# Channel mixing by Strassen's seven block products, with the activations in DRAM

## The chip, the cores and the metric

One core of a Trainium2 chip runs the whole kernel in one launch. The metric is the device time of one execution in microseconds (us). TensorE (PE) multiplies; VectorE (DVE), ScalarE (ACT) and GpSimd (POOL) do the elementwise work; the queue of SyncE (SP) issues most transfers.

## The reference, cut to what matters

One decoder layer for 1024 tokens of width 1024. The change concerns the second half, after the residual add of the mixing part:

```
x = x + gt1[:, None, :] * (merged @ w_out[l])
h2 = _modulate(x, norm2_g[l], sh2, sc2)
ff_out = jnp.square(jax.nn.relu(h2 @ w_ff1[l])) @ w_ff2[l]
x = x + gt2[:, None, :] * ff_out
return _rmsnorm(x, final_g)
```

h2 is 1024 x 1024, w_ff1 1024 x 4096 ("up"), w_ff2 4096 x 1024 ("down"), everything in float32.

## The kernel before, in words

Every float32 product is made of three fp32r matmuls: each operand is split into a high part (hi, an ACT cast) and a low part (lo = raw - hi, a DVE subtraction), and PE adds hi·hi, lo·hi and hi·lo in PSUM. An operand tile so costs one ACT and one DVE operation.

The mixing half fills the first 1036 us. Its last step is w_out: for each of eight token blocks t, 96 matmuls into `p_out`, then DVE forms x1 = x + gt1 * p_out in tile `xr`, SP stores it to `x1_d` in DRAM, ACT squares it, a chain of small operations (`rsqrt`, seven DVE and ACT operations on one column) gives the row scale, DVE scales `xr`, and after four blocks PE transposes (`hp`), ACT applies the conditioning (`hr`) and each 128x512 piece is split into `hhi` and `hlo`: h2 transposed, kept in SBUF.

The channel half goes by 32 column blocks n of 128. `up(n)` loads a block of w_ff1 (`load_w`, split into wh and wl), multiplies (48 matmuls of 512 columns), and makes relu squared as a split pair `fh`, `fl`. `w2(n)` loads the matching 128 rows of w_ff2, POOL multiplies them by gt2, and ACT and DVE split them. `down(g)` takes two n at a time (four in the last) and for each token block and each half of the columns adds the products of n in one PSUM bank `o`; DVE adds it to `acc[t]`, which was loaded with x1. In the last group `finish(t)` normalises a block as soon as it is complete and stores it. Ups and downs alternate in program order, two ups ahead. Each engine runs its instructions in the order in which the scheduler has put them.

## Time and profile before

| | |
|---|---|
| median of 3 runs | 1753.14 us (1746.7 to 1756.55) |
| profiled execution, its own time | 1749.61 us |
| its span in the trace | 1747.6 us |
| PE busy | 1671.4 us, 96% |
| DVE busy | 971.1 us, 56% |
| ACT busy | 570.3 us, 33% |
| POOL busy | 368.3 us, 21% |
| first up matmul / last down matmul begins | 1036.9 / 1739.40 us |

The times of single operations come from the profiled execution, 3.5 us under the median. Busy shares are means over the whole span; those of a stretch are read from the windows below.

### The profile page before, as it was taken

How to read it: one execution, taken by the hardware profiler on the slowest of the kernel's cores; microseconds unless marked ns; L12 is line 12 of the kernel's file. 1: busy time of each engine (PE TensorE's matmuls, PEld its weight loads, DVE VectorE, ACT ScalarE, POOL GpSimd, SP SyncE). 2: the span in 40 equal slices, each digit the busy share in tenths (PEclk: the TensorE clock that was granted, in tenths of full speed). 3: DMA queues.
4: the chain of work that ended last, by engine and by line, in shares of the span. 5: the costliest groups of instructions: out<-in, count | busy, mean ns of one | idle time of the engine just before them, and what ended most of it. 6: DMA issues, size and time to landing. Idle time of an engine off the chain costs nothing.

```text
span 1747.6 us, 21804 instructions
## 1 busy us (share of the span) xinstructions
PE 1671.4 (96%) x8677; PEld 1350.8 (77%) x8677; DVE 971.1 (56%) x1500; ACT 570.3 (33%) x869; POOL 368.3 (21%) x265
## 2 busy tenths in 40 slices
...
GB/s 249 126 112 154 109 99 161 121 61 61 67 70 103 73 232 240 249 235 232 248 204 247 75 125 137 49 48 49 48 49 49 49 49 49 48 49 48 37 12 96
DMA packets 205907, 197.50 MB, mean 113 GB/s; under 512 B 28113, under 2 KB 170730, under 8 KB 205678
## 3 DMA queue, kind: packets, MB, share of 16 engines
...
q10 hardware_dynamic: 208, 0.28, 0.0%
HBM read 148.80 MB, written 43.09 MB: 110 GB/s over the span
## 4 chain that ended last, share of the span: by engine, by line
PE 81%; DVE 5%; DMA 4%; ACT 2%; issue 1%; POOL 0%; SPq 0%; DVEq 0%; ACTq 0%
PE o L41 20%; PE p_f L41 20%; PE p_gb L41 5%; PE p_out L41 4%; PE p_ga L41 3%; PE my L41 3%; PE p_ob L41 2%; PE p_fq L41 2%; PE p_fv L41 2%; PE p_fk L41 2%; PE p_v L41 2%; PE yv L41 2%; PE p_r L41 2%; PE p_k L41 2%; PE tp L818 2%; PE s L41 1%
## 5 line engine op out<-in xcount | busy, mean ns | idle before, releaser
L1193 DVE TENSOR_TENSOR acc<-acc,o 128x512 f32<-128x512 f32 x240 | 162.1, 686 | 193.8 <-PE o L41 193.8
L1157 POOL TENSOR_TENSOR w2r<-w2r,gt 128x1024 f32<-128x1024 f32 x32 | 77.3, 2431 | 721.8 <-DMA w2r<-in_w_ff 721.7
L41 PE MATMUL p_f<-hlo,wh_f 128*128 128x512 f32 x512 | 200.0, 391 | 0.0
L41 PE MATMUL p_f<-hhi,wl_f 128*128 128x512 f32 x512 | 199.6, 390 | 0.0
L41 PE MATMUL p_f<-hhi,wh_f 128*128 128x512 f32 x512 | 199.5, 390 | 0.0
L41 PE MATMUL o<-w2h,fl 128*128 128x512 f32 x496 | 193.4, 390 | 0.0
L41 PE MATMUL o<-w2l,fh 128*128 128x512 f32 x496 | 193.2, 390 | 0.0
L41 PE MATMUL o<-w2h,fh 128*128 128x512 f32 x496 | 193.0, 389 | 0.0
L1143 ACT ACTIVATE rl<-p_f 128x1024 f32<-128x1024 f32 x32 | 32.9, 1028 | 268.4 <-PE p_f L41 268.4
L177 DVE TENSOR_TENSOR wl_f<-wr_f,wh_f 128x1024 fp32r<-128x1024 f32 x32 | 41.1, 1284 | 142.3 <-ACT wh_f L176 142.3
L1163 ACT CAST w2h<-w2r 128x1024 fp32r<-128x1024 f32 x31 | 31.1, 1050 | 251.4 <-PE o L41 251.4
L41 PEld LDWEIGHTS p_f<-hlo,wh_f 128*128 128x128 f32 x512 | 96.1, 188 | 20.4 <-DVE hlo L1124 0.5
L41 PEld LDWEIGHTS p_f<-hhi,wl_f 128*128 128x128 f32 x512 | 96.1, 188 | 20.2
L41 PEld LDWEIGHTS p_f<-hhi,wh_f 128*128 128x128 f32 x512 | 96.1, 188 | 20.0
L41 PEld LDWEIGHTS o<-w2h,fl 128*128 128x128 f32 x496 | 93.1, 188 | 20.0
L41 PEld LDWEIGHTS o<-w2h,fh 128*128 128x128 f32 x496 | 93.1, 188 | 19.8
L41 PEld LDWEIGHTS o<-w2l,fh 128*128 128x128 f32 x496 | 93.1, 188 | 19.5
L638 POOL TENSOR_TENSOR dg<-dg,inv 128x62 f32<-128x62 f32 (+30 forms) x62 | 100.2, 1616 | 4.8
L637 POOL TENSOR_TENSOR inv<-dg 128x62 f32<-128x62 f32 (+30 forms) x62 | 93.0, 1500 | 4.9
L822 DVE TENSOR_TENSOR pl<-tp,ph 128x512 fp32r<-128x512 f32 (+1 forms) x80 | 49.2, 632 | 24.8 <-ACT ph L821 24.6
L700 POOL TENSOR_TENSOR sw<-sbd,wcs 64x256 f32<-64x256 f32 x28 | 22.9, 818 | 168.0 <-DVE sbd L701 137.5
L880 ACT ACTIVATE pt<-pt,sm 128x128 f32<-128x128 f32 (+3 forms) x64 | 49.5, 775 | 24.5 <-DVE sm L878 23.5
...
## 6 DMA issues: line engine op xcount, KB each, us to landing
...
```

The source lines that it names most:

```text
L41: PE.matmul(o, l, r, start=start, stop=stop)
L177: DVE.tensor_tensor(lo, raw, hi.bitcast(F32), ALU.subtract)
L637: POOL.tensor_tensor(tv, dg[:, 0:s, s : s + 1].broadcast_to([P, s, m]), dg[:, s : s + 1, s + 1 :].broadcast_to([P, s, m]), ALU.mult)
L638: POOL.tensor_tensor(dg[:, 0:s, s + 1 :], dg[:, 0:s, s + 1 :], tv, ALU.add)
L700: POOL.tensor_tensor(sw[rs], cur[rs, :, rs], wcs[rs, :, c : c + 1].broadcast_to([64, 4, 64]), ALU.mult)
L818: PE.transpose(tp[:, x * P : (x + 1) * P], pr[b][:, t * P : (t + 1) * P], ident)
L822: DVE.tensor_tensor(pl[:, 0:w_], tp[:, 0:w_], ph[:, 0:w_].bitcast(F32), ALU.subtract)
L880: ACT.activation(pt[:, 0:n], pt[:, 0:n], AF.Exp, bias=low, scale=-1.0, accum_out=ls[:, b : b + 1])
L1143: ACT.activation(rl, o, AF.Relu)
L1157: POOL.tensor_tensor(raw, raw, gt2, ALU.mult)
L1163: ACT.copy(wh, raw)
L1193: DVE.tensor_tensor(acc[t][:, sl], acc[t][:, sl], o, ALU.add)
```

## The change

Strassen's scheme in Winograd's form splits each matrix product into 2 x 2 blocks and makes seven block products in place of eight, for sums of blocks before and after.

**Up.** The 32 column blocks go in 16 pairs j. The inner dimension is cut in two halves of four 128-row tiles, the tokens in two halves, the pair in its two blocks. On the side of h2 four sums T1 to T4 are built once, for each k of four by three POOL and three DVE sums and five splits (`t0` to `t3`, `hx`, and T3 and B22 written over parts of hhi and hlo). On the side of the weights each pair needs S1 to S4 (four POOL sums of 128x512) and seven splits. A pair takes 7 x 12 = 84 matmuls for 96. Four result blocks `ff0` to `ff3` of a pair, 128x512, are put together from PSUM banks x, y, z by ACT copies and DVE adds, go through relu squared, and are stored to `f_d` in DRAM. The products that need only h2's first token half (`up_first`, x and z) are issued around the sums T.

**Down.** After all ups, four groups g of eight column blocks go through seven steps each. A step is one block product: four token blocks t, 12 matmuls of 512 columns each. Four A blocks (activations, from `f_d`) and four B blocks (w_ff2), 128x2048 each (1 MB), are loaded per group, each tile once per group; POOL makes S1 to S4 and T1 to T4 at 128x2048, and each step splits its two operands (slots for two steps). Results go from PSUM to `acc` (the first time by an ACT copy, later by DVE). gt2 and x1 are applied to acc in the last group (`close_half`), then `finish`.

The diff, cut to its core; code of w_out that has only moved is left out:

```diff
+    def raw_pair(j):
+        tiles = []
+        for d in range(2):
+            if j % 3 == 0:
+                r = wp.tile([P, 4, 2 * P], F32, tag="wraw", name=f"ur{j}_{d}", bufs=2)
+            else:
+                r = dpr.tile([P, 4, 2 * P], F32, tag="dr", name=f"ur{j}_{d}", bufs=4)
+            SP.dma_start(r, ff1[:, 4 * d : 4 * d + 4, 2 * P * j : 2 * P * (j + 1)])
+            tiles.append(r)
+        return tiles
...
+    def split(hi, lo, src):
+        ACT.copy(hi, src)
+        DVE.tensor_tensor(lo, src, hi.bitcast(F32), ALU.subtract)
...
+        if t == 3:
+            for k in range(KT):
+                hp_ = turn(0, k, "ps")
+                hr = dpr.tile([P, 512], F32, tag="dr", name=f"hr2{t}_{k}", bufs=4)
+                ACT.activation(hr, hp_, AF.Identity, bias=sh2[:, k : k + 1], scale=sc2[:, k : k + 1])
+                split(hhi[:, k, 0:512], hlo[:, k, 0:512], hr)
+            raw1[0] = raw_pair(0)
+            for d in (1, 0):
+                first_ops(0, d)
...
+    psum_pools(x=(4, 512), y=(2, 512), z=(2, 512))
+    hxh, hxl = [hx.tile([P, 3, 4, 512], F32R, name=f"hx{x}") for x in "hl"]
+    blk = lambda t_, d, g: t_[:, 4 * d : 4 * d + 4, 512 * g : 512 * g + 512]
+    HB = {
+        "B11": (blk(hhi, 0, 0), blk(hlo, 0, 0)),
+        "B21": (blk(hhi, 1, 0), blk(hlo, 1, 0)),
+        "B22": (blk(hhi, 1, 1), blk(hlo, 1, 1)),
+        "T3": (blk(hhi, 0, 1), blk(hlo, 0, 1)),
...
+    def up_product(o, w, b, start):
+        (wh, wl), (bh, bl) = w, HB[b]
+        for k in range(4):
+            mmx(o, wh[:, k], bh[:, k], start and k == 0, False)
+            mmx(o, wl[:, k], bh[:, k], False, False)
+            mmx(o, wh[:, k], bl[:, k], False, k == 3)
...
+    def f_store(j, b, sq=None):
+        f = Fb[j, b]
+        DVE.scalar_tensor_tensor(f, f, 0.0, f, ALU.max, ALU.mult)
+        SP.dma_start(f_d[b, j], f)
...
+            z = bank(f"z{j}", "z")
+            up_product(z, (wh[:, 4:8], wl[:, 4:8]), "B21", True)
+            ACT.copy(f_tile(j, 0), z)
+        else:
+            X[j] = bank(f"x{j}", "x")
+            up_product(X[j], (wh[:, 0:4], wl[:, 0:4]), "B11", True)
+            DVE.tensor_tensor(Fb[j, 0], X[j], Fb[j, 0], ALU.add)
+            f_store(j, 0)
...
+    for k in range(4):
+        hr = dpr.tile([P, 2, 512], F32, tag="dr", name=f"hr3{k}", bufs=4)
+        for i in range(2):
+            hp_ = turn(4, k + 4 * i, "y")
+            ACT.activation(hr[:, i], hp_, AF.Identity, bias=sh2[:, k + 4 * i : k + 4 * i + 1], scale=sc2[:, k + 4 * i : k + 4 * i + 1])
+        h12, h22 = hr[:, 0], hr[:, 1]
+        tt = [tq.tile([P, 512], F32, name=f"t{x}_{k}", tag=f"hxt{x}", bufs=1) for x in range(4)]
+        f32 = lambda b, i: HB[b][i][:, k].bitcast(F32)
+        DVE.tensor_tensor(tt[0], h12, f32("B11", 0), ALU.subtract)
+        DVE.tensor_tensor(tt[0], tt[0], f32("B11", 1), ALU.subtract)
+        POOL.tensor_tensor(tt[2], h22, h12, ALU.subtract)
+        split(HB["T1"][0][:, k], HB["T1"][1][:, k], tt[0])
+        DVE.tensor_tensor(tt[1], h22, tt[0], ALU.subtract)
+        split(HB["T2"][0][:, k], HB["T2"][1][:, k], tt[1])
+        split(HB["B22"][0][:, k], HB["B22"][1][:, k], h22)
+        POOL.tensor_tensor(tt[3], f32("B21", 0), tt[1], ALU.subtract)
+        POOL.tensor_tensor(tt[3], tt[3], f32("B21", 1), ALU.add)
+        split(HB["T3"][0][:, k], HB["T3"][1][:, k], tt[2])
+        split(HB["T4"][0][:, k], HB["T4"][1][:, k], tt[3])
+        up_first(k // 2, k % 2 == 0)
+    tops.close()
...
+        made = {
+            "S1": (a21, a22, ALU.add),
+            "S2": (src, a11, ALU.subtract),
+            "S4": (a12, src, ALU.subtract),
+            "S3": (a11, a21, ALU.subtract),
+        }.get(name)
+        if made:
+            POOL.tensor_tensor(src, *made)
+        wh, wl = [up_.tile([P, 4, P], F32R, name=f"{name}{x}_{j}", tag=f"wop{x}", bufs=5) for x in "hl"]
+        split(wh, wl, src)
+        rest[j, name] = wh, wl
...
+        if i == 0:
+            y = X[j, "y"] = bank(f"y{j}", "y")
+            up_product(y, rest.pop((j, "S1")), "T1", True)
+            ACT.copy(f_tile(j, 3), y)
+        elif i == 1:
+            up_product(x, rest.pop((j, "S2")), "T2", False)
+            ACT.copy(f_tile(j, 1), x)
+        elif i == 2:
+            up_product(X[j, "y"], rest.pop((j, "S4")), "B22", False)
+            DVE.tensor_tensor(Fb[j, 1], X[j, "y"], Fb[j, 1], ALU.add)
+            f_store(j, 1)
+        elif i == 3:
+            up_product(x, rest.pop((j, "S3")), "T3", False)
+            DVE.tensor_tensor(Fb[j, 3], x, Fb[j, 3], ALU.add)
+            f_store(j, 3)
+        else:
+            up_product(x, rest.pop((j, "A22")), "T4", False)
+            ACT.activation(f_tile(j, 2), x, AF.Relu)
+            f_store(j, 2)
...
+    for j in range(NPAIR):
+        if j + 2 < NPAIR:
+            raw1[j + 2] = raw_pair(j + 2)
+        for i in range(5):
+            if i == 4 and j + 2 < NPAIR:
+                up_first(j + 2, True)
+            up_step(j, i)
+            if j + 1 < NPAIR:
+                rest_op(j + 1, ORDER[i])
+            if j + 2 < NPAIR and i in (1, 2):
+                first_ops(j + 2, 2 - i)
+        if j + 2 < NPAIR:
+            up_first(j + 2, False)
...
-        def up(n):
-            o = proj(load_w(ff1[:, :, n * P : (n + 1) * P], 0, KT, f"f{n}"), f"p_f{n}")
-            rl = fp.tile([P, S], F32, name=f"rl{n}", tag="rl", bufs=2)
-            ACT.activation(rl, o, AF.Relu)
-            if n < NFF - 1:
-                fh = fp.tile([P, S], F32R, name=f"fh{n}", tag="fh", bufs=3)
-                fl = fp.tile([P, S], F32R, name=f"fl{n}", tag="fl", bufs=3)
-            else:
-                fh, fl = [wp.tile([P, S], F32R, name=f"f{x}{n}", tag="wraw", bufs=2) for x in "hl"]
-            ACT.activation(fh, rl, AF.Square)
-            DVE.tensor_tensor(rl, rl, rl, ALU.mult)
-            DVE.tensor_tensor(fl, rl, fh.bitcast(F32), ALU.subtract)
-            return fh, fl
-        def w2(n):
-            raw = fp.tile([P, D], F32, name=f"w2r{n}", tag="w2r", bufs=2)
-            SP.dma_start(raw, ff2[n])
-            POOL.tensor_tensor(raw, raw, gt2, ALU.mult)
-            if n < NFF - 1:
-                wh = fp.tile([P, D], F32R, name=f"w2h{n}", tag="w2h", bufs=3)
-                wl = fp.tile([P, D], F32R, name=f"w2l{n}", tag="w2l", bufs=3)
-            else:
-                wh, wl = [wp.tile([P, D], F32R, name=f"w2{x[-1]}{n}", tag=x, bufs=2) for x in ("whi", "wlo")]
-            ACT.copy(wh, raw)
-            DVE.tensor_tensor(wl, raw, wh.bitcast(F32), ALU.subtract)
-            return wh, wl
...
+            t_ = raws[name] = fp.tile([P, 4, 512], F32, name=f"{name}_{g}", tag=name, bufs=1)
+            i = int(name[2])
+            if name[0] == "A":
+                b = {"11": 0, "12": 2, "21": 1, "22": 3}[name[1:]]
+                src = f_d[b, 4 * g : 4 * g + 4].rearrange("j p n -> p j n")
+            else:
+                n, d = {"11": (0, 0), "12": (0, 1), "21": (1, 0), "22": (1, 1)}[name[1:]]
+                src = ff2[:, 8 * g : 8 * g + 8].rearrange("p (j i) n -> p j i n", i=2)[:, :, n, 512 * d : 512 * d + 512]
+            SP.dma_start(t_, src)
...
+                POOL.tensor_tensor(R["S"], R["A21"], R["A22"], ALU.add)
...
+        STEPS = [
+            ("y", True, "A12", "B21", [(0, 0)]),
+            ("x", True, "A11", "B11", [(0, 0)]),
+            ("y", True, "S", "T", [(1, 1)]),
+            ("x", False, "S", "T", [(0, 1)]),
+            ("y", False, "S", "B22", [(0, 1)]),
+            ("x", False, "A21", "B12", [(1, 1)]),
+            ("x", False, "A22", "T", [(1, 0)]),
+        ]
+        SUMS = [(), (), ("S1", "T1"), ("S2", "T2"), ("S4",), ("S3", "T3"), ("T4",)]
+        LOADS = [("A12", "B21"), ("A11", "B11"), ("A21", "A22", "B12"), ("B22",), (), (), ()]
...
+                hi, lo = [fp.tile([P, 4, 512], F32R, name=f"{x}{y}{g}_{i}", tag=f"op{x}{y}", bufs=2) for y in "hl"]
+                split(hi, lo, raws[name])
...
+            if (t, d) in seen:
+                DVE.tensor_tensor(acc[t][:, sl], o, acc[t][:, sl], ALU.add)
+            else:
+                seen.add((t, d))
+                ACT.copy(acc[t][:, sl], o)
...
+            x1t = fp.tile([P, 512], F32, name=f"x1t{t}_{d}", tag="x1t", bufs=4)
+            SP.dma_start(x1t, x1_d[t][:, sl])
+            a_ = acc[t][:, sl]
+            DVE.tensor_tensor(a_, a_, gt2[:, sl], ALU.mult)
+            DVE.tensor_tensor(a_, a_, x1t, ALU.add)
+            jk = fp.tile([P, 512], F32, name=f"jk3{t}{d}", tag="jk3", bufs=1)
+            ACT.activation(jk, a_, AF.Square, accum_out=ssq[:, 8 * d + t : 8 * d + t + 1])
...
-                    o = bank(f"o{g}_{t}_{hf}")
-                    for i in range(n):
-                        (fh, fl), (wh, wl) = fs[i], ws[i]
-                        mm(o, fh[:, ts_], wh[:, sl], i == 0, False)
-                        mm(o, fl[:, ts_], wh[:, sl], False, False)
-                        mm(o, fh[:, ts_], wl[:, sl], False, i == n - 1)
-                    DVE.tensor_tensor(acc[t][:, sl], acc[t][:, sl], o, ALU.add)
...
+        flat = [(g, i) for g in range(NG) for i in range(7)]
+        operands(*flat[0])
+        for s, (g, i) in enumerate(flat):
+            if s + 1 < len(flat):
+                operands(*flat[s + 1])
+            tag, opens, _, _, to = STEPS[i]
+            (fh, fl), (wh, wl) = ops.pop((g, i))
+            for t in range(4):
+                ts_ = slice(t * P, t * P + P)
+                if opens:
+                    banks[tag, t] = bank(f"{tag}{g}_{i}_{t}", tag)
+                o = banks[tag, t]
+                for j in range(4):
+                    mmx(o, fh[:, j, ts_], wh[:, j], opens and j == 0, False)
+                    mmx(o, fl[:, j, ts_], wh[:, j], False, False)
+                    mmx(o, fh[:, j, ts_], wl[:, j], False, j == 3)
+                for half, d in to:
+                    evict(o, t + 4 * half, d)
+                if g == NG - 1:
+                    if i == 4:
+                        close_half(t, 0)
+                        close_half(t, 1)
+                        finish(t)
+                    elif i == 5:
+                        close_half(t + 4, 1)
+                    elif i == 6:
+                        close_half(t + 4, 0)
+                        finish(t + 4)
```

In program order PE has the same rows as before up to the last p_out matmul but for the names of transposes; in all it has 7007 rows for 7391. Three places in the order, `L` being the line in each kernel's own file:

DVE, before, from the scaling of the last token block on; `hr27_k` is the k-th piece of the second token half, then the splits of weights and activations of the first ups follow:

```order
L1113 TENSOR_SCALAR xr7_8978<-xr7_8978,rs2_8407 128x1024
L1124 TENSOR_TENSOR hlo_125<-hr27_0_8998,hhi_124 128x512
L1124 TENSOR_TENSOR hlo_125<-hr27_1_9007,hhi_124 128x512
...
L1124 TENSOR_TENSOR hlo_125<-hr27_7_9061,hhi_124 128x512
L177 TENSOR_TENSOR wl_f2_9231<-wr_f2_9228,wh_f2_9230 128x1024
L1150 TENSOR_TENSOR rl0_9145<-rl0_9145 128x1024
```

DVE, after, from the same place on, then the end of that stretch; `hr3k` holds two pieces, `S1l_0` is the low part of the first S1 of pair 0, on which the first matmul into bank `y0` waits:

```order
L1153 TENSOR_SCALAR xr7_8994<-xr7_8994,rs2_8413 128x1024
L1234 TENSOR_TENSOR t0_0_9054<-hr30_9041,hhi_124 128x512
L1235 TENSOR_TENSOR t0_0_9054<-t0_0_9054,hlo_125 128x512
L1238 TENSOR_TENSOR t1_0_9055<-hr30_9041,t0_0_9054 128x512
L1104 TENSOR_TENSOR hlo_125<-hr30_9041,hhi_124 128x512
L1104 TENSOR_TENSOR hxl_9029<-t0_0_9054,hxh_9028 128x512
L1104 TENSOR_TENSOR hlo_125<-t2_0_9056,hhi_124 128x512
L1104 TENSOR_TENSOR hxl_9029<-t1_0_9055,hxh_9028 128x512
...
L1104 TENSOR_TENSOR uwlo2_9310<-ur2_0_9265,uwhi2_9309 128x512
L1104 TENSOR_TENSOR hxl_9029<-t1_3_9200,hxh_9028 128x512
L1104 TENSOR_TENSOR hxl_9029<-t3_3_9202,hxh_9028 128x512
L1104 TENSOR_TENSOR S1l_0_9243<-S_0_9240,S1h_0_9242 128x512
```

Where eight subtractions for hlo stood ahead of the first weight split, 38 rows now stand up to and with `S1l_0`; one of them is an add from PSUM, the other 37 take both inputs from SBUF.

POOL, before, in the channel half: one row for each n, 32 in all, of which these are the first:

```order
L1157 TENSOR_TENSOR w2r0_9214<-w2r0_9214,gt2_5349 128x1024
L1157 TENSOR_TENSOR w2r1_9221<-w2r1_9221,gt2_5349 128x1024
L1157 TENSOR_TENSOR w2r2_9480<-w2r2_9480,gt2_5349 128x1024
L1157 TENSOR_TENSOR w2r3_9487<-w2r3_9487,gt2_5349 128x1024
L1157 TENSOR_TENSOR w2r4_9746<-w2r4_9746,gt2_5349 128x1024
```

POOL, after, from the first sum of the down part on; `S1_0` and `T1_0` are the slots in which S1, S2, S4 and T1, T2, T4 of group 0 follow each other:

```order
L1342 TENSOR_TENSOR S1_0_11529<-A21_0_11523,A22_0_11525 128x2048
L1353 TENSOR_TENSOR A21_0_11523<-A11_0_11455,A21_0_11523 128x2048
L1345 TENSOR_TENSOR T1_0_11531<-B12_0_11527,B11_0_11457 128x2048
L1355 TENSOR_TENSOR B12_0_11527<-B22_0_11597,B12_0_11527 128x2048
L1347 TENSOR_TENSOR S1_0_11529<-S1_0_11529,A11_0_11455 128x2048
L1349 TENSOR_TENSOR T1_0_11531<-B22_0_11597,T1_0_11531 128x2048
L1357 TENSOR_TENSOR T1_0_11531<-B21_0_11445,T1_0_11531 128x2048
L1351 TENSOR_TENSOR S1_0_11529<-A12_0_11443,S1_0_11529 128x2048
L1345 TENSOR_TENSOR T1_1_11989<-B12_1_11985,B11_1_11915 128x2048
```

In group 0 the sum S3 (written over A21) and the sum T3 (over B12) stand ahead of S2 and T2; eight sums of 128x2048 a group take the place of eight multiplications of 128x1024.

SP, after, between the last store of the up part and the loads of group 0 (before, the loads of w_ff1 and w_ff2 alternate to the end, two blocks ahead):

```order
L1201 DMA f_d_9030<-ff3_15_11352 128x512
L1201 DMA f_d_9030<-ff2_15_11410 128x512
L1335 DMA A12_0_11443<-f_d_9030 128x4x512
L1335 DMA B21_0_11445<-in_w_ff2 128x4x512
L1335 DMA A11_0_11455<-f_d_9030 128x4x512
L1335 DMA B11_0_11457<-in_w_ff2 128x4x512
L1335 DMA A21_0_11523<-f_d_9030 128x4x512
L1335 DMA A22_0_11525<-f_d_9030 128x4x512
L1335 DMA B12_0_11527<-in_w_ff2 128x4x512
L1335 DMA B22_0_11597<-in_w_ff2 128x4x512
```

All eight loads of group 0 now stand behind the last activation's store, which waits for DVE's relu-square of the last up product.

## Rows read from the trace of the kernel before

**Rows 1.** The page: busy time of PE, and the chain that ended last.

```profile
span 1747.6 us, 21804 instructions
PE 1671.4 (96%) x8677; PEld 1350.8 (77%) x8677; DVE 971.1 (56%) x1500; ACT 570.3 (33%) x869; POOL 368.3 (21%) x265
...
PE 81%; DVE 5%; DMA 4%; ACT 2%; issue 1%; POOL 0%; SPq 0%; DVEq 0%; ACTq 0%
```

**Rows 2.** Busy time by stretch in the channel half, granted clock (PEclk) near the end.

```profile
core 0: us, PE busy (x) PEld busy (x) DVE busy (x) ACT busy (x) POOL busy (x), PEclk, DMA share, GB/s
1100.00:1200.00 100.00, 100.00 (x442) 82.66 (x441) 43.43 (x51) 18.63 (x19) 14.32 (x6) 1.00 0.17 53
```

**Rows 3.** Groups by line and shape from 960 us to the end: busy us, mean ns.

```profile
L1193 DVE TENSOR_TENSOR acc<-acc,o 128x512 f32<-128x512 f32 x240 | 162.1, 686 | 193.8 <-PE o L41 193.8
L1157 POOL TENSOR_TENSOR w2r<-w2r,gt 128x1024 f32<-128x1024 f32 x32 | 77.3, 2431 | 721.8 <-DMA w2r<-in_w_ff 721.7
L1163 ACT CAST w2h<-w2r 128x1024 fp32r<-128x1024 f32 x31 | 31.1, 1050 | 251.4 <-PE o L41 251.4
L1122 ACT ACTIVATE hr<-hp,sh,sc 128x512 f32<-128x512 f32 x16 | 11.7, 789 | 6.6 <-PE hp L1120 6.6
L1124 DVE TENSOR_TENSOR hlo<-hr,hhi 128x512 fp32r<-128x512 f32 x16 | 10.4, 688 | 12.0 <-ACT hhi L1123 12.0
L1123 ACT CAST hhi<-hr 128x512 fp32r<-128x512 f32 x16 | 9.2, 635 | 0.0
L1120 PE MATMUL hp<-ident,xr 128*128 128x128 f32 x64 | 9.6, 278 | 0.3 <-DVE xr L1113 0.3
L1178 DVE SCALAR_TENSOR_TENSOR acc<-acc,rs,gt 128x1024 f32<-128x1024 f32 x7 | 9.0, 1280 | 0.0
```

**Rows 4.** Timeline of POOL, then of DVE, from 1056 us on: start, length.

```profile
1057.18 5.75 POOL L1157 TENSOR_TENSOR w2r<-w2r,gt 128x1024 f32<-128x1024 f32 x2 [186.12 <-DMA w2r<-in_w_ff]
...
1057.54 3.12 DVE L177 TENSOR_TENSOR wl_f<-wr_f,wh_f 128x1024 fp32r<-128x1024 f32 x1 [2.76 <-ACT wh_f L176]
1060.59 3.42 DVE L1150 TENSOR_TENSOR rl<-rl 128x1024 f32<-128x1024 f32 x1
1064.05 1.22 DVE L1151 TENSOR_TENSOR fl<-rl,fh 128x1024 fp32r<-128x1024 f32 x1
```

**Rows 5.** DVE groups from 300 to 510 us; L822 reads PSUM (`tp`).

```profile
L822 DVE TENSOR_TENSOR pl<-tp,ph 128x512 fp32r<-128x512 f32 x29 | 19.3, 685 | 11.8 <-ACT ph L821 11.8
...
L177 DVE TENSOR_TENSOR wl_fv<-wr_fv,wh_fv 128x1024 fp32r<-128x1024 f32 x3 | 8.5, 2820 | 0.3 <-ACT wh_fv L176 0.3
```

**Rows 6.** POOL's adds of 128x512 at L719: ns min/median/max.

```profile
L719 POOL TENSOR_TENSOR bv<-bv,lnb x8: 1278/1292/2144, 633.0 to 838.4; 128x512 f32<-128x512 f32 x8
```

**Rows 7.** Timeline of DVE around the last p_out matmul.

```profile
1036.27 1.23 DVE L1108 TENSOR_TENSOR t<-p_out,gt 128x1024 f32<-128x1024 f32 x1 [0.48 <-PE p_out L41]
...
1043.19 0.75 DVE L1113 TENSOR_SCALAR xr<-xr,rs 128x1024 f32<-128x1024 f32 x1 [1.42 <-DMA x_d<-xr]
```

**Rows 8.** Timeline of the kernel's end, all engines.

```profile
1739.40 0.40 PE L41 MATMUL o<-w2o,fh 128*128 128x512 f32 x1
...
1741.37 0.16 DVE L1174 TENSOR_TENSOR ssq<-ssq 128x1 f32<-128x1 f32 x1 [0.85 <-ACT jk L1196]
...
1742.86 1.41 DVE L1178 SCALAR_TENSOR_TENSOR acc<-acc,rs,gt 128x512 f32<-128x512 f32 x2
```

**Rows 9.** Timeline of SP and ACT at the start (loads of 0.5 MB), and a window.

```profile
0.81 1.34 SPq L233 DMA_DIRECT2D x<-in_x  x3
...
4.29 1.06 ACT L261 ACTIVATE jk<-x 128x1024 f32<-128x1024 f32 x1 [0.56 <-DMA x<-in_x]
...
4.00:8.00 4.00, 0.28 (x1) 0.18 (x1) 0.12 (x2) 2.45 (x5) 0.00 (x0) 1.00 0.95 368
```

**Rows 10.** Windows of 2 us where PE starts again.

```profile
220.00:222.00 2.00, 0.94 (x5) 0.95 (x6) 2.00 (x3) 0.00 (x0) 0.00 (x0) 0.69 0.64 224
222.00:224.00 2.00, 2.00 (x11) 2.00 (x10) 0.25 (x1) 1.17 (x2) 0.00 (x0) 0.50 0.12 38
```

More of the change, by code (lines that the diff above doesn't have):

```diff
@@ L1073, in build @@
             pass
+        dpr = mix.enter_context(pool(name="dpr", bufs=1, side="right"))
         dpa = dax.enter_context(pool(name="dpa", bufs=1, side="right"))
-        raws = [wo_load(dpa, k) for k in range(4)]
+        raws = [wo_load(dpr, k) for k in range(4)]
         for j, _ in enumerate(merge_a(yp, gp, ready, 1)):
@@ new lines, in split, with first_ops @@
+    def split(hi, lo, src):
+        ACT.copy(hi, src)
+        DVE.tensor_tensor(lo, src, hi.bitcast(F32), ALU.subtract)
+    raw1, first = {}, {}
+    def first_ops(j, d):
+        if d:
+            first[j] = [wp.tile([P, KT, P], F32R, tag=tag, name=f"u{tag}{j}", bufs=2) for tag in ("whi", "wlo")]
+        ks = slice(4 * d, 4 * d + 4)
+        split(first[j][0][:, ks], first[j][1][:, ks], raw1[j][d][:, :, 0:P])
+    px = tops.enter_context(pool(name="px", bufs=1))
+    dps = ExitStack()
+    dp = dps.enter_context(pool(name="dp", bufs=1))
@@ new lines, in f_tile, with up_first @@
+    def f_tile(j, b):
+        Fb[j, b] = upool().tile([P, 512], F32, name=f"ff{b}_{j}", tag=f"ff{b}", bufs=1 if b == 2 else 2)
+        return Fb[j, b]
+    def up_first(j, which):
+        wh, wl = first[j]
+        if which:
+            z = bank(f"z{j}", "z")
[6 more added lines that the diff above has]
+            f_store(j, 0)
```

191 lines of the change are left out of this document (115 added, 76 removed).

## The prediction

> **What bounds it now.** I read the page first: PE is busy for 1671.4 of 1747.6 us and holds 81% of the chain that ended last [rows 1]. The windows of the channel half show PE at 100.00 of 100 us with 442 matmuls, clock 1.00, and DVE at 43, ACT at 19, POOL at 14 us [rows 2]: a matmul of 512 columns costs 100/442 = 0.2265 us there, and nothing else costs anything. So whatever takes matmuls away pays in full, as long as the other engines and the loads keep up; the question is where they don't. The groups by shape then give the price of each elementwise form [rows 3], and the timelines what happens where two engines meet [rows 4].
>
> **What is taken away.** PE has 7391 - 7007 = 384 fewer rows: 16 pairs x 12 in up, 4 groups x 4 x 12 in down. 384 x 0.2265 = **-87.0 us**.
>
> **How DVE and POOL stand to each other.** This decides most of the rest. While POOL multiplied twice from 1057.18 to 1062.93, DVE's subtraction and square took 3.12 and 3.42 us; the next operation of the same size, with POOL idle, took 1.22 [rows 4]. End to end the four took 6.83 us; alone they need 2 x 2.43 + 2 x 1.22 = 7.3 [rows 3, 4]. They ran one after the other. Between 300 and 510 us, when POOL is busy nearly throughout, the weight split took 2820 ns, but the operation that reads one input from PSUM stayed at 685 for 128x512 [rows 5], which is also its price elsewhere (686, the adds to acc [rows 3]). So I count time of POOL sums and of DVE operations with two SBUF inputs as one queue, and evictions from PSUM as free of it.
> The Trainium skill, "SBUF — State Buffer", section "Who interferes with whom", has this as a rule: a DVE operation with two SBUF inputs and a GpSimd one that reads SBUF hold a shared pair of ports by an exclusive lock, whichever comes first, for the whole instruction. The trace agrees (3.12 against 1.22 us). By the rule the sum below is +21; without it -26.
>
> **Start of up.** The last p_out is read at 1036.27 and xr7 is scaled at 1043.19 + 0.75 = 1043.94 [rows 7]; before, PE filled that time with the first half of the first ups. Now two splits of pair 1's weights and a relu-square (about 0.69 each) have slipped into that chain on DVE: take +1.7, so 1045.6. Transposes and the conditioning (0.79 [rows 3]) follow, and T starts at about 1047.5. Then the first matmul into y0 needs S1l_0, and the order puts 37 DVE operations with two SBUF inputs up to it and with it, and 13 POOL sums. DVE: 36 x 0.65 = 23 us (0.69 a piece [rows 3], overlapping a little back to back). POOL: 13 x 1.29 = 16.8 [rows 6]. One queue: 40 us, y0 at 1087. PE has, from 1036.3 on, 60 matmuls (x0, z0, x1, z1, x2: 13.6 us) and 32 transposes (0.15 each [rows 3]: 4.8), so of 51 us it idles 33: **+33**. If the two overlap freely DVE alone, with its waits for ACT, sets y0 at about 1072: +17.
>
> **Up, steady.** A pair takes 84 x 0.2265 = 19.0 us of PE. POOL has 4 x 1.29 = 5.2, DVE 7 x 0.65 and 4 relu-squares with both inputs in SBUF (4 x 0.65) and three PSUM adds (2.1): 9.3; the shared queue holds 12.4, ACT seven casts and four copies, 11 x 0.635 = 7.0 [rows 3]. Loads and stores are 2 MB in 19 us, 110 GB/s, where 368 was seen [rows 9]. All of it lies under PE: 0. If the cover were gone a pair would have to grow by 6.6 us on the shared queue before it showed.
>
> **Up to down.** No down work is ready when the last up matmul ends: every load of group 0 stands on SP behind the last store, which waits for a relu (0.63) and a relu-square (0.69): issue at 1.75. A load of 0.5 MB was issued at 0.81 and used at 4.29 [rows 9]; 0.5 MB at 368 GB/s is 1.4 us, so 2.1 us lie around it, and a load of 1 MB is there 2.1 + 2.85 after its issue, the next ones each 2.85 later. A12 lands at 6.7, B21 at 9.6. The trace has no split of 128x2048: DVE 1.22 for 1024 columns [rows 4] and 0.69 for 512 [rows 3], so by the slope 2.29 (estimate); ACT 1.05 [rows 3] gives 1.85 to 2.1; POOL 1.29 [rows 6] and 2.43 [rows 3] give 4.71 (twice 2.43 would be 4.86). The cast of B21 ends at 11.5, its low part at 13.8, needed a few matmuls in: PE effectively starts at 12.65. Steps 0 and 1 end at 34.4. Step 2 needs S1 and T1. A21 and A22 have landed at 20.9, then POOL makes S1, S3, T1 (14.1), with the low part of S1 between (2.29): T1 at 37.3. Its low part waits behind T3 (4.71): 44.3, wanted about 1 us into the step, a stall of 8.9. S2 then ends at 49.0, T2 at 53.7, their low parts at 56.0 and 58.3 or behind T4; step 3, due at 54.2, loses about 5.0. S4 stands behind T4: it ends near 67.7, and a cast and two low parts follow, about 75 for a step due at 70: 4.8. **+31**; without the shared queue, T1's low part at 39 and no waits for T4, 22.5.
>
> The Trainium skill, "GPSIMD Engine Reference", section 3.1 on elementwise cycles, gives 4497 ns on GpSimd and 2293 on VectorE for a tensor_tensor of this size; no run here shows it yet. By that the sum would shift by less than 1 us in a group.
>
> **Groups 1 to 3.** A group is 336 x 0.2265 = 76.1 us of PE. The shared queue holds 8 x 4.71 + 14 x 2.29 = 69.7; 6 us are left. But the steps up to 3 want six sums (28.3) and eight low parts (18.3) within four steps (43.5), 3 over, and a low part can stand behind one more sum (4.7). I take 4 a group, **+12**; bounds 0 (no queue, or all prepared ahead) and 18. The loads have a group's time: 8 x 2.85 = 23 of 76.
>
> **Tail.** Before, the span ends 1747.6 - 1739.8 = 7.8 us after the last matmul, of which 3.3 are the last store [rows 8]. Now the last group carries all closings. From the end of step 4's first block on DVE has 12 evictions, 16 multiplications by gt2 and 16 adds of x1 (44 x 0.67 = 29.5 us), eight finishes of 1.49 (1741.37 to 1742.86) and 1.28 (22.2) [rows 3, 8], two low parts for step 6 behind step 4's closings (4.6), and before each finish a wait for the last Square, of which the next half's work leaves about 0.5: 4. That is 60, from 2.7 us into step 4, where PE has 32.6 for steps 4 to 6. With the last store the end is 60 + 2.7 + 3.3 = 66 after step 4 begins, against 32.6 + 7.8 = 40.4, and most of a last sum (T4 or S4, 4.7) falls between: **+29**; 18 if no wait is left and step 6's low parts come ahead of the closings.
>
> **Clock.** PE stood idle until about 221; then the granted clock was 0.69 and then 0.50 (1.2 GHz of 2.4) over two windows of 2 us [rows 10]: 2 x 0.31 + 2 x 0.50 = 1.6 us lost. The new gaps at the start of up and of down each meet that: **+3**.
>
> **Sum.** -87 + 33 + 31 + 12 + 29 + 3 = +21 on the profiled execution's 1749.6: **1771 us**. The median is 3.5 above that execution; the spread of the three runs, 10 us, is wider than that, so I leave it out. Faster or slower by 0.5% (8.75 us) is what a measurement can tell here.
>
> **Rivals.**
> *R1, the other side: DVE and POOL do not hold each other up here.* For it: sums and splits differ in shape from those of [rows 4], and the adds from PSUM are seen untouched [rows 5]. Against it: 3.12 for 1.22. Then -87 + 17 + 22.5 + 0 + 18 + 3 = -26: 1723. It decides if DVE's 128x512 operations at the start of up stay under about 0.75 us each. Chance 0.16.
> *R2, one queue, but better interleaved:* evictions and waits on ACT fill the gaps, groups 1 to 3 cost 2, group 0 24, the tail 22, clock 2: -87 + 33 + 24 + 2 + 22 + 2 = -4, 1746. For it: PSUM evictions (28 x 0.69 = 19 us of 51 in a group) can lie beside POOL's sums. Chance 0.23.
> *R3, loads at half the rate:* rows of 2 KB in blocks of 1 MB, 5.7 us each. S1 in group 0 waits for the sixth load, 6 x 2.85 = 17 more; the later groups hide 46 in 76. 1788. For it: the loads of [rows 9] have longer rows. Against: nothing in the windows shows a limit. Chance 0.09.
> *That the change does not do what it says* is excluded for the matmuls by the order of PE; chance 0.
> My forecast holds 0.52, its own range 1755 to 1788.
>
> **Range and chances.** 1730 to 1795 leaves out most of R1 and little of R3. Faster: R1 and 0.09 of R2, 0.25. Same: 0.13 of R2 and 0.05 of the forecast's low end, 0.18. Slower: 0.57.
>
> **What would show it.** In the profile after: 128x512 subtractions in the T stretch well over 0.69 where POOL is busy, y0's first matmul some 50 us after the last p_out; then windows at 100% in up; a gap of 12 us and stalls in group 0, POOL's 128x2048 near 4.7; small stalls after; the last store more than 20 us behind the last matmul's own time. The prediction is wrong if PE's matmul pace changes under the 2 MB per pair, or if the T stretch lasts under 30 us.

## The result: 1.0% slower, and where the time went

The changed kernel takes 1772.05 us (median of 7 runs, 1768.18 to 1777.1), the kernel before 1754.94 in the 7 runs beside it: ratio 1.0102, 95% interval 1.0075 to 1.013. The forecast was 1771. The profiled execution took 1768.18 us, its span is 1766.5, that is 18.9 more than before. The first half of the program, which is not changed, ended in the profiled executions of this study anywhere between 1035 and 1046 us; so I compare stages, counted from the last p_out matmul, and medians only where they differ by more than that. As to the spread of a stage: where an edit leaves it alone, the up stage (last p_out to last up matmul) took 351.4 to 352.7 us in six executions, and the part from there to the end 379.3 to 380.7 in five.

The page of the changed kernel, the lines that answer to [rows 1]:

```profile
span 1766.5 us, 21676 instructions
PE 1615.5 (91%) x8293; PEld 1291.3 (73%) x8293; DVE 1113.6 (63%) x1564; ACT 664.9 (38%) x1001; POOL 594.5 (34%) x341
...
PE 57%; DVE 12%; POOL 9%; DMA 6%; issue 6%; ACT 3%; SPq 0%; DVEq 0%; POOLq 0%; ACTq 0%
```

PE has the 384 matmuls less, but it is idle for 9% of the span where it was idle for 4%, and DVE, POOL and DMA stand in the chain with 27% together, where they had 9%. The timeline of PE shows the stages: the last p_out, the first y0, the last matmul of up, the first of each down group, the last of all.

```profile
1035.11 0.39 PE L41 MATMUL p_out<-l_wo,hhi 128*128 128x512 f32 x1
...
1081.72 0.51 PE L1185 MATMUL y<-hxh,S1h 128*128 128x512 f32 x1 [0.40 <-ACT S1h L1103]
...
1387.20 0.39 PE L1185 MATMUL x<-hxl,A22h 128*128 128x512 f32 x1
1399.32 0.79 PE L1185 MATMUL y<-wh,fh 128*128 128x512 f32 x1 [11.73 <-ACT wh L1103]
...
1493.73 0.39 PE L1185 MATMUL y<-wh,fh 128*128 128x512 f32 x1
...
1578.26 0.39 PE L1185 MATMUL y<-wh,fh 128*128 128x512 f32 x1
...
1661.11 0.39 PE L1185 MATMUL y<-wh,fh 128*128 128x512 f32 x1
...
1750.23 0.39 PE L1185 MATMUL x<-wl,fh 128*128 128x512 f32 x1
```

A stage's loss is its length less its matmuls at 0.2265 us (and 32 transposes at 0.15):

| stage | length | matmul time | lost | forecast, clock included |
|---|---|---|---|---|
| up, from the last p_out to the last up matmul | 352.1 | 309.2 | 42.9 | 33 + 1.5 |
| group 0, 1387.20 to 1493.73 | 106.5 | 76.1 | 30.4 | 31 + 1.5 |
| groups 1 and 2, to 1661.11 | 167.4 | 152.2 | 15.2 | 8 |
| group 3 and tail, to 1766.5, less the 7.8 of before | 105.4 | 76.1 | 21.5 | 4 + 29 |

The losses add to 110.0; with -87.0 that is +23. The same reckoning for the kernel before gives 703.6 us from its last p_out to its last matmul for 700.6 us of work, so 3 us of loss that are gone, and its last p_out came 0.7 later: +19, the 18.9 of the spans. The total of the forecast was right within 2 us, but two terms were 7 to 8 too small and one 11 too large.

Whom PE waited for, from the first up product to the last, and then from there to the end (us in total, times, longest):

```profile
PE x L1185 <- ACT uwhi L1103: 13.6, 1, 13.6
PE hp L1128 <- ACT hr L1230: 6.5, 3, 2.5
PE x L1185 <- DVE ff L1287: 5.8, 2, 5.0
PE x L1185 <- DVE uwlo L1104: 3.6, 1, 3.6
...
PE y L1185 <- DVE fl L1104: 13.3, 7, 2.3
PE y L1185 <- ACT wh L1103: 13.0, 2, 11.7
PE x L1185 <- DVE fl L1104: 4.8, 2, 3.0
PE y L1185 <- DVE wl L1104: 4.1, 1, 4.1
```

Behind the 11.7 are the first loads of group 0 and their casts; behind most of the others in down are DVE and POOL. First the groups of DVE by shape in the down part (busy us, mean ns): low parts of 2.29 us, alone, became 2.37 to 3.81 on the mean of a group, while the adds from PSUM stayed at 683 (686 before [rows 3]). Then POOL's sums there: of the eight kinds only the T3 sum keeps 4.61.

```profile
L1104 DVE TENSOR_TENSOR wl<-B,wh 128x2048 fp32r<-128x2048 f32 x16 | 61.0, 3810 | 7.3 <-ACT wh L1103 7.3
L1104 DVE TENSOR_TENSOR fl<-A,fh 128x2048 fp32r<-128x2048 f32 x16 | 49.8, 3110 | 8.1 <-ACT fh L1103 8.1
L1391 DVE TENSOR_TENSOR acc<-x,acc 128x512 f32<-128x512 f32 x56 | 36.2, 683 | 13.8 <-PE x L1185 13.8
...
L1104 DVE TENSOR_TENSOR fl<-S,fh 128x2048 fp32r<-128x2048 f32 x12 | 28.4, 2368 | 28.4 <-ACT fh L1103 28.4
...
L1357 POOL TENSOR_TENSOR T<-B,T 128x2048 f32<-128x2048 f32 x4 | 26.3, 6576 | 16.3 <-DVE wl L1104 16.3
...
L1355 POOL TENSOR_TENSOR B<-B,B 128x2048 f32<-128x2048 f32 x4 | 18.4, 4611 | 0.3
```

6576 is 4.61 and most of a low part, 3810 is 2.29 and a part of a sum: each waits out the other.

### The profile page after: what moved, and what is told of

Its sections match the earlier page's. It is cut to its first block, busy times and chain, and to the rows that moved or that the text cites. A ratio compares the mean times of both kernels' runs of the same rounds, so it can differ in the third digit from the quotient of the medians.

```text
span 1766.5 us, 21676 instructions
## 1 busy us (share of the span) xinstructions
PE 1615.5 (91%) x8293; PEld 1291.3 (73%) x8293; DVE 1113.6 (63%) x1564; ACT 664.9 (38%) x1001; POOL 594.5 (34%) x341
## 4 chain that ended last, share of the span: by engine, by line
PE 57%; DVE 12%; POOL 9%; DMA 6%; issue 6%; ACT 3%; SPq 0%; DVEq 0%; POOLq 0%; ACTq 0%
PE x L1185 10%; PE y L1185 7%; PE p_gb L41 4%; PE p_out L41 4%; PE p_ga L41 3%; PE p_fk L41 2%; PE z L1185 2%; PE p_fq L41 2%; PE p_fv L41 2%; PE my L41 2%; PE p_ob L41 2%; PE p_v L41 2%; PE yv L41 2%; PE p_r L41 2%; PE tp L819 2%
## 5 line engine op out<-in xcount | busy, mean ns | idle before, releaser
L1185 PE MATMUL x<-wh,fl 128*128 128x512 f32 x256 | 101.2, 395 | 4.8 <-DVE fl L1104 4.8
L1185 PE MATMUL x<-wh,fh 128*128 128x512 f32 x256 | 101.3, 396 | 2.0 <-DVE rtmp L158 1.5
L1185 PE MATMUL x<-wl,fh 128*128 128x512 f32 x256 | 100.8, 394 | 0.0
L1185 PE MATMUL y<-wh,fh 128*128 128x512 f32 x192 | 80.5, 419 | 13.8 <-ACT wh L1103 13.0
L1185 PE MATMUL y<-wh,fl 128*128 128x512 f32 x192 | 79.9, 416 | 13.3 <-DVE fl L1104 13.3
L1185 PE MATMUL y<-wl,fh 128*128 128x512 f32 x192 | 79.4, 414 | 4.1 <-DVE wl L1104 4.1
L701 POOL TENSOR_TENSOR sw<-sbd,wcs 64x256 f32<-64x256 f32 x28 | 22.9, 817 | 170.1 <-DVE sbd L702 138.0
L1200 DVE SCALAR_TENSOR_TENSOR ff<-ff 128x512 f32<-128x512 f32 x64 | 58.2, 909 | 33.3 <-ACT ff L1291 33.1
L1104 DVE TENSOR_TENSOR wl<-B,wh 128x2048 fp32r<-128x2048 f32 x16 | 61.0, 3810 | 7.3 <-ACT wh L1103 7.3
L1185 PEld LDWEIGHTS x<-wh,fl 128*128 128x128 f32 x256 | 48.9, 191 | 15.6 <-DVE fl L1104 5.5
L1103 ACT CAST wh<-T 128x2048 fp32r<-128x2048 f32 x12 | 22.9, 1911 | 98.1 <-issue 32.1
L879 DVE CUSTOM_DVE_ANT_0 pt<-s,cb 128x512 f32<-128x512 f32 (+2 forms) x64 | 36.3, 585 | 36.9 <-PE s L41 36.3
L1185 PEld LDWEIGHTS x<-wh,fh 128*128 128x128 f32 x256 | 48.7, 190 | 13.4 <-issue 1.9
L1185 PEld LDWEIGHTS y<-wh,fl 128*128 128x128 f32 x192 | 39.0, 203 | 24.3 <-DVE fl L1104 15.9
```

Source lines behind the costliest of these rows:

```text
L701: POOL.tensor_tensor(sw[rs], cur[rs, :, rs], wcs[rs, :, c : c + 1].broadcast_to([64, 4, 64]), ALU.mult)
L879: DVE.tensor_tensor_reduce(pt[:, c0:c1], sv, cb[:, c0:c1], -0.125, low, ALU.add, ALU.min, st_[:, x : x + 1])
L1103: ACT.copy(hi, src)
L1104: DVE.tensor_tensor(lo, src, hi.bitcast(F32), ALU.subtract)
L1185: PE.matmul(o, l, r, start=start, stop=stop, skip_group_check=True)
L1200: DVE.scalar_tensor_tensor(f, f, 0.0, f, ALU.max, ALU.mult)
```

## The experiments

Theory A: a POOL sum and a DVE operation with two SBUF inputs exclude each other, each for its whole length, and this makes most of the loss. Theory B: they run side by side, and what is lost is DVE's own work or the chain of dependences. Other rivals, with letters of their own, are named in the expectations. All runs start from the changed kernel.

**1. T sums on DVE** (`t_dve`).

```diff
-        POOL.tensor_tensor(tt[2], h22, h12, ALU.subtract)
+        DVE.tensor_tensor(tt[2], h22, h12, ALU.subtract)
...
-        POOL.tensor_tensor(tt[3], f32("B21", 0), tt[1], ALU.subtract)
-        POOL.tensor_tensor(tt[3], tt[3], f32("B21", 1), ALU.add)
+        DVE.tensor_tensor(tt[3], f32("B21", 0), tt[1], ALU.subtract)
+        DVE.tensor_tensor(tt[3], tt[3], f32("B21", 1), ALU.add)
```

> The twelve POOL sums that build T at the start of up are done by DVE. Theory A (a POOL sum and a DVE operation with two SBUF inputs exclude each other, so both lie in one queue): the stretch from the first T operation to the first y0 matmul, 36 us in the changed kernel, gets shorter by 12 x (1.28 - 0.61) = 8 us, 28 us, and the whole is 6 to 9 us faster than the changed kernel. Theory B (they run side by side, DVE's own work is what lasts): DVE has 12 x 0.61 = 7 us more to do in the stretch, 40 us or more, the whole 3 to 8 us slower than the changed kernel.

Measured: 1774.39 us, ratio 1.0123 (1.0094 to 1.0152) to the kernel before: no faster than the changed kernel, so A's 6 to 9 us did not come. Nor was either theory right by the measure of the expectation: from the first T operation to the first y0 matmul it took 35.1 us for 36.3, not 28 and not 40. What A has for it is DVE's own part: from the first T operation to the end of S1l_0 it took 31.2 us for 37.8, with twelve more operations on DVE: -6.6, against B. PE made little of it, since it stood at the weight split of x2, ahead of y0 (13.6 and 3.6 us before the edit):

```profile
PE x L1185 <- ACT uwhi L1103: 13.3, 1, 13.3
PE x L1185 <- DVE uwlo L1104: 6.1, 1, 6.1
```

The whole up stage is only 2.3 shorter (349.8). The S sums are still on POOL; run 9, which moves them too, gains 11.3 more. POOL's timeline here:

```profile
1063.44 19.62 POOL L1267 TENSOR_TENSOR S<-ur,ur 128x512 f32<-128x512 f32 x1 [184.06 <-PE hp L1128]
1083.14 1.61 POOL L1267 TENSOR_TENSOR ur<-ur 128x512 f32<-128x512 f32 x1
1087.18 1.28 POOL L1267 TENSOR_TENSOR S<-S,ur 128x512 f32<-128x512 f32 x1 [2.43 <-DVE S1l L1104]
```

A sum of 1.28 us stood for 19.62 us, while DVE ran its T operations one behind the other without a gap. A was right on DVE's part and wrong on the whole, since I had not counted what PE waits for beside it and after it.

**2. Down sums on DVE** (`down_dve`): the eight `POOL.tensor_tensor` of down_sum become `DVE.tensor_tensor`.

```diff
-                POOL.tensor_tensor(R["S"], R["A21"], R["A22"], ALU.add)
+                DVE.tensor_tensor(R["S"], R["A21"], R["A22"], ALU.add)
```

> The eight sums of 128x2048 of each down group are done by DVE (2.29 us each) instead of POOL (4.61). Theory A: one queue of 8 x 4.61 + 14 x 2.29 = 69 us becomes 22 x 2.29 + 28 x 0.61 = 67 on DVE with no exclusion; a single sum is 2.3 us shorter and its follower never waits 4.6, so the stalls of steps 0 and 4 in groups 1 to 3 (about 4.2 each with the clock) shrink to under 1.5 each and steps 2 to 4 of group 0 (15 us) lose about half: 20 to 28 us faster than the changed kernel. Theory B: DVE's work in a group rises from 51 to 69 of 76 us for nothing: no change or up to 10 us slower.

Measured: 1732.11 us, ratio 0.989 (0.9859 to 0.9922) to the kernel before; from the last up matmul to the end 340.1 us for 379.3 (-39.2, more than A expected). Every step from group 0's step 1 to the last group's step 5 follows the one before without a loss. PE's waits in the whole down part:

```profile
PE y L1185 <- ACT wh L1103: 12.0, 1, 12.0
PE x L1185 <- DVE acc L1391: 3.1, 1, 3.1
```

The low parts are back at their length alone (DVE groups of this run), though DVE now does 22 instead of 14 operations of this size in a group:

```profile
L1104 DVE TENSOR_TENSOR wl<-B,wh 128x2048 fp32r<-128x2048 f32 x16 | 36.6, 2287 | 7.1 <-ACT wh L1103 7.1
```

B is out: DVE had 18 us more work a group, and the group got shorter. What this run leaves open is whether exclusion or just the shorter sum did it; run 5 tells that.

**3. Early loads** (`early`): A12 and B21 live in the four buffers of the up weights as two halves each, and group 0's are issued before the last pair; splits and the sums S4 and T4 go by halves.

```diff
+        if j == NPAIR - 1:
+            early["A12"] = halves(0, "A12", f_d[2, 0:4].rearrange("j p n -> p j n"))
+            early["B21"] = halves(0, "B21", ff2[:, 0:8].rearrange("p (j i) n -> p j i n", i=2)[:, :, 1, 0:512])
...
-                split(hi, lo, raws[name])
+                    for q in range(2):
+                        split(hi[:, 2 * q : 2 * q + 2], lo[:, 2 * q : 2 * q + 2], raws[name][q])
```

> A12 and B21 are kept in the four buffers of the up weights, so that in group 0 they are loaded during the last up pair. Theory A: the loss of 15.0 us before step 0 falls to 5 or 6 (two casts and a low part remain); the six other loads are still issued after the last store, the first sum's operand lands about 5.7 us earlier, so step 2 loses some 3 more than its 8.7: 5 to 7 us faster than the changed kernel. Theory L (the opening loads alone are what group 0 lacks): step 2 loses no more than now: 9 to 10 us faster.

Measured: 1783.13 us, ratio 1.017 (1.0129 to 1.0212), slower than both; the down part 393.0 for 379.3. Step 0 lost 5.5 for 15.0 as both theories said, and step 2 3.1 more, as A said; but step 0 of groups 1 to 3 now lost 8.4 each (4.2, 2.6, 4.2 before the edit). DVE's timeline there shows why: three halves of 1.22 us took 15.9.

```profile
1481.29 4.73 DVE L1104 TENSOR_TENSOR wl<-B,wh 128x1024 fp32r<-128x1024 f32 x1 [0.17 <-ACT wh L1103]
1485.94 11.13 DVE L1104 TENSOR_TENSOR fl<-A,fh 128x1024 fp32r<-128x1024 f32 x2
```

POOL's timeline beside it:

```profile
1480.31 4.63 POOL L1374 TENSOR_TENSOR B<-B,B 128x2048 f32<-128x2048 f32 x1
1484.89 5.59 POOL L1361 TENSOR_TENSOR S<-A,A 128x2048 f32<-128x2048 f32 x1
1490.56 5.43 POOL L1372 TENSOR_TENSOR A<-A,A 128x2048 f32<-128x2048 f32 x1
```

Each half waits for a whole sum on POOL, so cutting an operation in two doubles its wait. The second operation, `fl`, took 6.70 us as a whole in the changed kernel and 11.13 in halves. Neither expectation had that.

**4. T1 first** (`t1_first`): S1 of pair 0 is made ahead of the T sums, T1 of all k ahead of the rest, and y0's product stands between.

```diff
+    POOL.tensor_tensor(s1, raw1[0][0][:, :, P:], raw1[0][1][:, :, P:], ALU.add)
+    split(s1h, s1l, s1)
...
+    X[0, "y"] = bank("y0", "y")
+    up_product(X[0, "y"], (s1h, s1l), "T1", True)
+    for k in range(4):
```

> S1 of pair 0 is made before the T sums, and the T1 chains of all four k come ahead of T2 to T4 in the program, so that fewer operations stand ahead of the first y0 matmul (26 DVE and 7 to 10 POOL operations for 37 and 13). Theory A: the amount of work in the one queue is the same, but PE gets y0 about 10 us sooner and x0's second product soon after the last T2; 4 to 8 us faster than the changed kernel, the rest comes back as waits for T2 to T4. Theory B (a chain of dependences, not the queue, sets the start): 12 us or more faster.

Measured: 1768.62 us, ratio 1.0088 (1.0058 to 1.0117); y0 27.8 us after the last p_out for 46.6, the up stage 346.2 for 352.1: -5.9. Of the 18.8 us that y0 gained (A had expected about 10), 12.9 came back behind it, so the stage gained what A expected, 4 to 8; B's 12 or more did not come.

**5. Low parts by ACT** (`lo_act`): ACT writes zeros where DVE subtracted, so this kernel leaves the low parts of the operands out of the down products; the matmuls stay.

```diff
-                split(hi, lo, raws[name])
+                ACT.copy(hi, raws[name])
+                ACT.activation(lo, raws[name], AF.Identity, scale=0.0)
```

> Down with the sums left on POOL, but the low parts of the operands are written as zeros by ACT instead of subtracted by DVE (this leaves the low parts out of the down products; the matmuls and their number stay). Theory A (mutual exclusion of POOL and two-input DVE work): POOL's eight sums a group each take 4.6 us with no delay, nothing blocks the operands, and the stalls of groups 1 to 3 (8.4, 6.7 and 8 us up to step 4) go to under 1; in group 0 step 2 loses 3 to 6 instead of 8.7 (three sums of 4.6 after the loads). Rival D (the sums are simply too long on POOL, 37 us a group, whoever runs beside them): the stalls stay within a third of what they are now.

Measured: 1733.83 us (one run); the down part 339.3 us, the same as with the sums on DVE (340.1). POOL made the same sums as in the changed kernel:

```profile
L1345 POOL TENSOR_TENSOR T<-B,B 128x2048 f32<-128x2048 f32 x4 | 18.5, 4615 | 79.3 <-ACT wl L1383 79.3
```

4615 for 6568 ns in the changed kernel, and no loss in groups 1 to 3; group 0 keeps 15.6 at step 0 and 4.6 at step 3 (A had expected 3 to 6 at step 2). So 37 us of sums in a group are not too long in themselves; D is out. What costs is that they and DVE's low parts cannot run at once. This run tells most. That its total equals run 2's is chance: it lost 5.8 more in group 0 and nothing at step 6 of the last group, where run 2 lost 6.1. What the two share is that groups 1 and 2 lose nothing.

**6. Early loads with the down sums on DVE** (`early_dve`): edits 2 and 3 together.

> Down sums on DVE and A12, B21 of group 0 loaded during the last up pair. In the run with down sums on POOL the early load gained 9.4 us at step 0 and lost more than that at the later steps, where the half-sized low parts let POOL in twice. Theory A: with no POOL work in down the halves cost nothing: step 0 loses 5 to 6 instead of 14.8, no stall comes back except up to 3 us at step 2, and the stages from the last up matmul on are 7 to 10 us shorter than with the down sums on DVE alone, 1721 to 1727. Rival E (the halves and the shared buffers themselves cost it): step 0 of groups 1 to 3 still loses 4 us or more each, no gain.

Measured: 1724.84 us, ratio 0.9831 (0.9774 to 0.9887); the down part 332.0 for 340.1, -8.1, step 0 loses 7.1 (5 to 6 expected) and no other step anything up to step 5 of the last group. With no POOL work beside them the halves cost nothing: E is out, and the loads at the opening are worth 8 us, as A had it.

**7. No closings** (`noclose_dve`): edit 2, without the lines of close_half that multiply, add and load.

```diff
-            DVE.tensor_tensor(a_, a_, gt2[:, sl], ALU.mult)
-            DVE.tensor_tensor(a_, a_, x1t, ALU.add)
```

> Down sums on DVE, and the 16 multiplications by gt2, 16 adds of x1 and their loads are left out at the end (the residual is then missing). If the tail is set by DVE's closings, the 6.1 us lost in steps 5 and 6 and 7 to 8 of the 14.3 us after the last matmul go: 9 to 14 us shorter from step 4 of the last group on. If it is set by the finishes and the last store, under 4.

Measured: 1719.39 us (one run); the down part 328.7 for 340.1, -11.4, and steps 5 and 6 lose nothing. The end after the last matmul begins is 9.5 us, 14.6 in run 2, where the kernel before has 8.2 by the same count. So the tail over before is the closings, nearly all of it.

**8. All of it** (`best`): all sums on DVE but the S1 of pair 0, which POOL makes before the T sums; T1 first, early loads.

> All sums on DVE (T, up and down), S1 of pair 0 and the T1 chains first, early load of A12 and B21. Theory A: the start has no exclusion any more, DVE has 49 operations of 0.61 us = 30 us in a row instead of 36 us in the mixed queue, y0 comes after about half of it; from the last p_out to the last up matmul 335 to 344 us instead of 352, and from there on as with the early load and down sums on DVE: 1710 to 1720 in all. Theory B: the start gets no shorter than with T1 first alone (346).

Measured: 1709.53 us, ratio 0.9742 (0.9686 to 0.9798) to the kernel before, 62 us under the changed kernel. The up stage takes 335.2 us, A's good end; B's 346 is out. Its DVE groups at the start have the low parts of T at their length alone, where the changed kernel's took 1163 ns:

```profile
L1104 DVE TENSOR_TENSOR hxl<-t,hxh 128x512 fp32r<-128x512 f32 x12 | 7.9, 688 | 0.1
```

**9 and 10. Which part of the start** (`tu_dve`: T and S sums on DVE, order as it was; `t1_first_dve`: edits 1 and 4, S sums on POOL). The first has this one edit more than run 1:

```diff
-            POOL.tensor_tensor(src, *made)
+            DVE.tensor_tensor(src, *made)
```

> T sums and the weight sums S of up on DVE, their order unchanged, down sums on POOL as in the changed kernel. From the last p_out to the last up matmul the changed kernel needs 352 us, T sums on DVE alone 350, T1 first alone 346, and all of it 335. Theory A (after the T stretch the S sums on POOL still alternate with DVE): 341 to 346, since the 20 POOL sums of the first five pairs no longer hold up the splits. Rival F (the gain of 335 comes from the order T1 first alone): 348 to 351.

> T1 first and T sums on DVE, S sums of up on POOL as in the changed kernel. Theory A: S2 and S4 of pair 0 on POOL have to wait for gaps in DVE's row of two-input operations, as one S sum did for 18 us with T sums on DVE alone; 339 to 344 us from the last p_out to the last up matmul. Rival F: 335 to 337, as with the S sums on DVE too.

Measured: up stages of 338.4 and 339.0 us (1762.85 and 1757.79 us, one run each). The first is 2.6 better than A's range and 10 from F's: F is out. The second lies at A's good end and 2.0 above F's, a small margin for one execution, and A's reason for it did not show: the three S sums of pair 0 that POOL made beside DVE's row were not shut out.

```profile
1059.07 2.71 POOL L1278 TENSOR_TENSOR S<-ur,ur 128x512 f32<-128x512 f32 x1 [22.12 <-ACT hxh L1103]
1061.86 1.59 POOL L1278 TENSOR_TENSOR S<-S,ur 128x512 f32<-128x512 f32 x1
1063.41 1.70 POOL L1278 TENSOR_TENSOR ur<-ur 128x512 f32<-128x512 f32 x1
```

Without T1 first, all sums on DVE give 13.7 of the 16.9 us, and T1 first with T on DVE but the S sums on POOL gives 13.1. Taking POOL out of T alone gave 2.3, out of T and S 13.7. That the exclusion goes on behind T as long as PE has no lead over the splits would fit this; no run shows it by itself.

## Why the prediction was right, step by step

- **Matmuls, -87.** Right: steps that wait for nothing take 10.88 us for 48 matmuls, 0.2267 each, as before.
- **DVE and POOL in one queue.** Shown: by the low parts and sums that lengthen each other, and by runs 2 and 5, which end it from either side: groups 1 and 2 lose nothing in either, for 15.2 us. PSUM evictions are free of it, 683 ns throughout. The Trainium skill, "SBUF — State Buffer", "Who interferes with whom", says just this, an exclusive lock between a GpSimd instruction that reads SBUF and a DVE instruction with two SBUF inputs, and none against one that reads SBUF once. The runs agree; but that whoever comes first has the lock did not hold in run 1, where a sum of 1.28 us stood for 19.62 while DVE went on. Not most of the loss, as theory A had it, but about half goes with it: 39.2 us in down (run 2) and 13.7 in up (run 9), 53 of 110, if the two add up. R1 is out: DVE's 128x512 operations at the start took up to 1.8 us, and its -26 would have needed them under 0.75.
- **Start of up, 33 + 1.5: too small by 8.** The price of the T stretch was about right, a little high: y0 came 46.6 us after the last p_out, for 51 forecast, and PE lost 28.4 of them to idle time and clock (46.6 less 59 matmuls and 32 transposes). The term that failed is the time behind y0, which I set to nothing, where 14.7 us went: 305.5 us for 1284 matmuls of 0.2265. Nor did PE stand at y0, as I had it, but most of the time at x2 (13.6 and 3.6 us of waits): x2's weights are loaded into the buffers of `hr3`, and SP waited 22.9 us until a T operation had released one:

```profile
SPq L1098 <- DVE t L1238: 23.1, 2, 22.9
```

  That wait lay beside the T stretch: y0 still waited 0.4 and 0.6 us for the split of S1. As to the 14.7, in it are a wait of 5.0 for the add of ff3 behind two splits that took 3.42 us beside POOL, the alternation of S sums and low parts (run 9), and the slow clock.
- **Up, steady, 0.** Right: between 1150 and 1375 PE is busy throughout.
- **Group 0, 31 + 1.5: right,** 30.4, and by parts: 15.0 at step 0 (12.65 forecast and the clock), 8.7, 3.8 and 2.8 (8.9, 5.0, 4.8).
- **Groups 1 and 2, 8: too small by 7.** The waits were sized right, two of 1.8 to 2.3 in a group for the 4 forecast, 8.2 in all. What was left out is the clock behind three of the four, which I had counted only at the two long gaps. Below are two of the waits on PE's timeline, which ended at 1496.38 and at 1580.92, and PE's windows around them (the last figures are granted clock, DMA share, GB/s):

```profile
1496.38 0.50 PE L1185 MATMUL y<-wh,fl 128*128 128x512 f32 x1 [2.27 <-DVE fl L1104]
...
1580.92 0.50 PE L1185 MATMUL y<-wh,fl 128*128 128x512 f32 x1 [2.27 <-DVE fl L1104]
```

The windows:

```profile
1494.00:1496.00 2.00, 0.12 (x1) 0.00 (x0) 2.00 (x1) 2.00 (x3) 1.92 (x2) 1.00 0.00 0
1496.00:1498.00 2.00, 1.62 (x6) 1.34 (x7) 2.00 (x2) 1.90 (x2) 2.00 (x1) 0.88 0.00 0
1498.00:1500.00 2.00, 2.00 (x6) 1.52 (x6) 2.00 (x1) 0.00 (x0) 2.00 (x1) 0.50 0.00 0
...
1580.00:1582.00 2.00, 1.08 (x5) 0.91 (x6) 2.00 (x4) 1.94 (x2) 2.00 (x1) 1.00 0.00 0
1582.00:1584.00 2.00, 2.00 (x11) 1.65 (x9) 2.00 (x4) 0.00 (x0) 2.00 (x1) 1.00 0.00 0
```

  After the first the granted clock stands at 0.50, 1.2 GHz, as in [rows 10], and the step loses 4.2 in all, wait included; after the second, as long, it stays at 1.00, and the step loses 2.6.
- **Group 3 and tail, 4 + 29: too large by 11**, the sum of two misses: up to step 4 the group lost 10.9 for 4, from step 5 on 10.4 for 29. I took the closings in the order of the source, all behind step 4. Half of a block is complete after step 1, and the scheduler had put its closing there: the first multiplications by gt2 stand in step 1 of the last group, on DVE's timeline, held up by POOL's sums:

```profile
1683.75 8.92 DVE L1402 TENSOR_TENSOR acc<-acc,gt 128x512 f32<-128x512 f32 x2
...
1699.41 2.29 DVE L1104 TENSOR_TENSOR fl<-S,fh 128x2048 fp32r<-128x2048 f32 x1
...
1761.75 1.42 DVE L1414 SCALAR_TENSOR_TENSOR acc<-acc,rs,gt 128x512 f32<-128x512 f32 x2
```

  The low parts of step 3 stand behind these closings, and that step lost 5.3. From step 4's first block on DVE was busy 46.1 us, where the forecast had 60: closings and evictions took 22.7 for 29.5, since eight of the 32 closings had gone ahead; the eight finishes 14.6 for 22.2, since their small operations ran between other work; the 4 of waits did not show; and four low parts took 8.8, where two were counted at 4.6. The order of DVE's instructions, which was to be had before the run, shows the first of these. The price of the closings was real: 11.4 us in run 7.
- **Prices by slope.** POOL 4.71 forecast, 4.61 measured; DVE 2.29 and 2.29.
- **R2 and R3.** R2 is out: the better interleaving that it wanted in groups 1 to 3, 2 us in all, was 15 in groups 1 and 2 alone. R3 is out: the loads of group 0 gave step 0 its forecast time, and the early load gained 8 to 9 us, not more.

The +21 came out at +19 in part by luck: errors of +8, +7 and -11 us offset each other. What was right is the mechanism, the matmul term and group 0.
